# Six weight buffers laid 96 bytes out of step in a hybrid decoder block

## The chip, the cores and the metric

The kernel runs on one core of a Trainium2 chip. The metric is the device time of one execution in microseconds: the median of three runs. TensorE (PE) multiplies; VectorE (DVE), ScalarE (ACT) and GpSimd (POOL) do the elementwise work; SyncE (SP), ACT and POOL issue DMA transfers. On-chip memory (SBUF) has 128 partitions, and each tile takes the same bytes of every partition, so an address here is a byte within a partition.

## The reference

One layer of a decoder for 512 tokens and 16 meta tokens of width 1024, all in float32. A normalised input goes through one wide projection; its parts feed a gated linear attention (GLA) and a state space layer (S5), whose outputs are gated, merged and projected; a squared-ReLU MLP follows.

```python
xn = rmsnorm(h, g_mix_pre[l])
proj = xn @ w_in[l]                       # 1024 x 6160
...
y_gla = o @ w_o_gla[l]
...
glu = g_s @ w_glu[l] + b_glu[l]
y_ssm = glu[..., :D_MODEL] * jax.nn.sigmoid(glu[..., D_MODEL:])
mixed = jax.nn.sigmoid(z_gla) * y_gla + jax.nn.sigmoid(z_ssm) * y_ssm
h = h + rmsnorm(mixed @ w_out[l], g_mix_post[l])
hn = rmsnorm(h, g_ffn_pre[l])
f = jnp.square(jax.nn.relu(hn @ w_ff1[l])) @ w_ff2[l]
h = h + rmsnorm(f, g_ffn_post[l])
```

## The kernel before

Most products are done in three passes of TensorE's one-pass float32 type (`float32r`): each operand is split into a high part and a remainder, and `mm3` adds high x high, high x remainder and remainder x high into one PSUM bank. The weights go through a chain of three kinds of buffers, three of each, in the pool `wp`: a DMA on SP brings a block of 4 KB per partition into `wraw`, ScalarE rounds it into `whi` (`split_hi`), VectorE subtracts and writes the remainder to `wlo`. A block is 8 x 128 columns of a weight matrix (`raw_w`, `split_w_hi`, `split_w_lo`, `load_w`), or, in the last stage, 2 x 512 (`operands`).

PE works on such a block in one of two ways.

- *Weights held.* `feat_tile` calls `mm3` with `whi[:, k]` or `wlo[:, k]`, 128 columns, as the operand that is loaded into the array (LDWEIGHTS in the profile) and streams the inputs past it: `rh`/`rl` (the first u projections), `xh`/`xl` (the rest of the input projection), `ogh`/`ogl` (GLA output), `gh`/`gl` (S5's GLU), `hh`/`hl` (MLP, first product). The order per k is `whi` with the high part, `whi` with the remainder, `wlo` with the high part. A matmul streams 512 columns, or 256 and 272 where the tokens go in two halves (`HALVES`).
- *Weights moving.* In the MLP's second product (`step`, `product`) the activations `fh`/`fl` are held and 512 columns of `whi` or `wlo` stream past.

`w_out` has buffers of its own (`woh`, `wol`) and takes only `wraw` from the chain.

Where a tile lies follows from its pool. `wp` is the second pool on the left side of SBUF; all left-side pools opened later (`px`, `pg`, `pgl`'s counterpart `pw`, `pff`, `pw2` and others) lie above it, and the right-side pools grow down from the top. In pools made with `padded=True`, `mk` rounds every tile up to `LINE` = 64 floats, 256 bytes; `lead` and `tail` bring the two sides to a multiple of 256 at their start. In the program as built, the three `wraw`, the three `whi` and the three `wlo` buffers follow each other at distances of exactly 4096 bytes and all start at a multiple of 256. So do `xh`, `xl`, `ogh`, `ogl`, `gh`, `gl`, `hh`, `hl`, `mh`, `ml`, `woh`, `wol`, `fh` and `fl`, and every slice of 128 columns or of one k in them. `rh` and `rl` start 192 bytes past a multiple of 256, and so does each of their k.

```python
LINE = 64
raw = mk(wp, [P, kt, P], tag="wraw", bufs=3)
hi = mk(wp, [P, raw.shape[1], P], F32R, tag="whi", bufs=3)
lo = mk(wp, [P, raw.shape[1], P], F32R, tag="wlo", bufs=3)
```

PE's order is mostly written out by hand (`pinned`), and around it the S5 and GLA work of the other engines is interleaved. POOL's queue carries DMAs that go around the core's DRAM, and in it, at line 812, the fill of `zpad` (zeros for a padded kernel table) and, at line 1552, the loads of `w2raw` (blocks of the second MLP matrix, of which VectorE forms sums for the last stage).

Of the kernel before, what the change touches and what calls it, by code (L numbers as in the profile page):

```python
# [9 lines left out]
F32 = mybir.dt.float32  # L10
F32R = mybir.dt.float32r
# [6 lines left out]
P = 128  # L18
D = 1024
KT = D // P  # L20
# [11 lines left out]
LINE = 64  # L32
# [18 lines left out]
def hybrid_block(ctx: ExitStack, tc: tile.TileContext, io, out: bass.AP):  # L51
# [17 lines left out]
    count = [0]  # L69
# [11 lines left out]
    def mk(pool, shape, dt=F32, tag=None, **kw):  # L81
        count[0] += 1
        name = f"{tag or 'x'}_{count[0]}"
        size = 1
        for n in shape[1:]:
            size *= n
        if pool not in lined or size % LINE == 0:
            return pool.tile(shape, dt, tag=tag or name, name=name, **kw)
        t = pool.tile([shape[0], -(-size // LINE) * LINE], dt, tag=tag or name, name=name, **kw)[:, :size]
        if len(shape) == 2:  # L90
            return t
        dims = " ".join("abcd"[: len(shape) - 1])
        return t.rearrange(f"p ({dims}) -> p {dims}", **dict(zip("abcd", shape[1:])))

    def f32(t):
        return t.bitcast(F32)

    def pool(name, bufs=1, space=None, stack=None, side="left", padded=False):
        kw = {"side": side} if space is None else {"space": space}
        if space != DRAM:  # L100
            kw["reuse_waits"] = "tile"
        made = (stack or ctx).enter_context(tc.tile_pool(name=name, bufs=bufs, **kw))
        if padded:
            lined.append(made)
        return made

    cst = pool("cst", padded=True)
    wp = pool("wp", padded=True)
    dr = pool("dr", space=DRAM)
    ps_mm = pool("ps_mm", bufs=4, space=PSUM)  # L110
# [48 lines left out]
    def split_hi(dst, src, scale=1.0):  # L159
        S.activation(dst, src, AF.Copy, scale=scale)  # L160

    def raw_w(src):

        kt, n = src.shape[0] // P, src.shape[1]
        raw = mk(wp, [P, kt, P], tag="wraw", bufs=3)
        return nc.sync.dma_start(raw[:, :, :n], src.rearrange("(k p) n -> p k n", p=P)), raw

    def split_w_hi(raw):
        hi = mk(wp, [P, raw.shape[1], P], F32R, tag="whi", bufs=3)
        split_hi(hi, raw)  # L170
        return hi

    def split_w_lo(raw, hi):
        lo = mk(wp, [P, raw.shape[1], P], F32R, tag="wlo", bufs=3)
        V.tensor_sub(lo, raw, f32(hi))  # L175
        return lo

    def split_w(raw):
        hi = split_w_hi(raw)
        return hi, split_w_lo(raw, hi)  # L180
# [298 lines left out]
    def busy(n, cols=256):  # L479

        for _ in range(n):
            PE.matmul(idle[:, :cols], ones[:, :P], ones[:, :cols], start=True, stop=True)
# [8 lines left out]
    for kind, i in (("h", 0), ("h", 4), ("a", 0), ("u", 2), ("x", 0), ("x", 1), ("x", 2), ("x", 3), ("x", 4), ("u", 3), ("u", 4), ("w", 0), ("g", 0), ("u", 5), ("c", 0), ("u", 6), ("u", 7)):  # L491
        with behind():
# [15 lines left out]
            else:  # L508
                loaded, raw = raw_w(w_in[:, C_U + i * P : C_U + (i + 1) * P])
# [82 lines left out]

    uts = [u_tile() for _ in range(3)] + [mk(qc, [P, T8, NCK], tag=f"ut{i}") for i in (3, 4)]
    busy(5)
    w0, w1 = (tuple(mk(wp, [P, KT, P], F32R, tag=t, bufs=3) for t in ("whi", "wlo")) for _ in range(2))
    for k in range(KT):
        taken_raw(k, 0)
        for w, raw in zip((w0, w1), raws):
# [33 lines left out]
    low(0, (0, 2))  # L632
    raw_product(w3, 0, pair2[:, 256:], (3, lambda: spreads.append(spread(1))))
    w4_hi = split_w_hi(raws[4])
    high(0, range(4, 8))
    rows_of(1, spreads[1])
    w4 = w4_hi, split_w_lo(raws[4], w4_hi)
    low(0, (4, 6))
    last[3] = bank()
# [26 lines left out]
    late_take(3, 0)  # L666
    late_take(3, 1)
    f1_hi = split_w_hi(raws[6])
    late_take(4, 0)
    f1 = f1_hi, split_w_lo(raws[6], f1_hi)  # L670
    late_take(4, 1)
    sx.close()
# [734 lines left out]
    for c in range(0, D, 256):  # L1407
# [11 lines left out]
        for i, w in enumerate(load_w(wg[:, c : c + 256])):  # L1419
# [3 lines left out]
            t = mk(pgl, [P, SEQ], tag="ti", bufs=2)  # L1423
# [16 lines left out]
    for k in range(KT):  # L1440
        raw = mk(wp, [P, D], tag="wraw", bufs=3)
# [70 lines left out]
    w1 = io["w_ff1"][0]  # L1512
# [13 lines left out]
    f = mk(pff, [P, MF, SEQ], tag="f")  # L1526
# [67 lines left out]
    def operands(a, b, jj):  # L1594
        raw = mk(wp, [P, 2, 512], tag="wraw", bufs=3)
        nc.sync.dma_start(raw, b)
        bh, bl = (mk(wp, [P, 2, 512], F32R, tag=t, bufs=3) for t in ("whi", "wlo"))
        halved = S.activation(bh, raw, AF.Copy)  # L1598
        if later and jj % 2:
            with tc.issue_after(halved.ins):  # L1600
                nc.scalar.dma_start(*later.pop(0))
        V.tensor_sub(bl, raw, f32(bh))  # L1602
        ah, al = (mk(pff, [P, 2, HT], F32R, tag=t, bufs=3) for t in ("fh", "fl"))
        split_hi(ah, a)
        V.tensor_sub(al, a, f32(ah))
        return ah, al, bh, bl
# [20 lines left out]
    def product(acc, a, b, first, beside=None, last=False, closes=False):  # L1627
        held = []
        for jj in range(NJ // 2):
            ops = operands(a(jj), b(jj), jj)  # L1630
            if beside:
                beside(jj)
            if last and jj >= NJ // 2 - 2:
                held.append(ops)
                continue
            for t in range(2):
                step(acc, t, ops, first and jj == 0, jj == NJ // 2 - 1)
        return held
# [105 lines left out]
```

## Time and profile before

| | before |
|---|---|
| median of 3 runs | 875.06 us (874.87 to 875.43) |
| the profiled execution | 874.97 us |
| its span on the core, first to last instruction | 873.2 us, mean granted TensorE clock 0.998 |
| PE matmul busy | 862.7 us, 4824 instructions |
| PE weight loads busy | 738.3 us, 4824 |
| VectorE / ScalarE / POOL busy | 654.6 / 442.4 / 121.4 us |

The rows of the profile are read so: a group row has line, engine, operation, out<-in, for PE the size of the array used and the shape of the output, the count, then busy time and mean duration of one in ns, and the engine's idle time ahead with what ended it. A timeline row has start in us, duration in us, and the same names. A matmul's duration runs into the next one, so the distance between two starts is the time that one takes of PE. PE busy means matmuls; PEld are weight loads, which run beside them.

The stages by time: first projections with `rh`/`rl` to 38 us; input projection with `xh`/`xl` among S5 and GLA work to about 360 us; GLA output, GLU and `w_out` to 538 us; the MLP's first product to 712 us; its second to the end.

### The profile page before, as it was taken

What the parts mean: (1) busy time and instruction counts of PE and PEld (TensorE: products, weight loads), DVE (VectorE), ACT (ScalarE), POOL (GpSimd) and SP (SyncE); (2) the same over time, 40 slices, a digit from 0 to 9 for tenths busy, and PEclk for the clock granted to TensorE, in tenths of its full rate; (3) what the DMA queues carried; (4) which work ended last, traced back from release to release, by engine and by line L of the source; (5) the groups of instructions that cost most, each with busy time, mean ns of one, the idle gap of its engine ahead of it and who ended that gap; (6) DMA issues with size and microseconds to landing.
All of it is one profiled execution on the core that took longest, in us unless ns stands there. A gap on an engine that the chain in (4) does not pass through costs nothing.

```text
span 873.2 us, 13275 instructions
## 1 busy us (share of the span) xinstructions
PE 862.7 (99%) x4824; PEld 738.3 (85%) x4824; DVE 654.6 (75%) x1181; ACT 442.4 (51%) x749; POOL 121.4 (14%) x213
## 2 busy tenths in 40 slices
PE   9999999999999999999999999999999999999996
PEld 8998889898988888888888889888888888888884
DVE  7999889979686699855446656576766677688886
ACT  7677456676763554334333544333222236665763
POOL 1123021130303222241000001011111100000001
PEclk9999999999999999999999999999999999999999
DMA  9777766545455747658545842498989966755464
GB/s 315 235 228 230 209 140 162 168 137 158 113 145 160 242 133 208 209 151 298 155 147 174 238 132 100 142 352 291 320 289 341 320 224 232 272 195 198 169 199 140
DMA packets 166905, 180.57 MB, mean 207 GB/s; under 512 B 18056, under 2 KB 126760, under 8 KB 166840
## 3 DMA queue, kind: packets, MB, share of 16 engines
q1 hardware_dynamic: 146832, 115.95, 44.6%
q0 software_dynamic: 17744, 58.52, 19.8%
q10 hardware_dynamic: 2264, 5.25, 1.9%
q8 instruction: 38, 0.62, 0.3%
q14 instruction: 27, 0.22, 0.1%
HBM read 143.74 MB, written 35.95 MB: 206 GB/s over the span
## 4 chain that ended last, share of the span: by engine, by line
PE 95%; DVE 3%; ACT 1%; issue 0%; ACTq 0%; DVEq 0%
PE mm L61 70%; PE sm L61 23%; PE sm L66 2%; DVE wlo L79 1%; DVE M L79 0%; DVE c L1665 0%; ACT whi L79 0%; DVE xT L79 0%; ACTq L79 0%; ACT vs L79 0%; DVE vs L79 0%; DVE c L1659 0%; DVE d L79 0%; DVE mta L79 0%; ACT L79 0%
## 5 line engine op out<-in xcount | busy, mean ns | idle before, releaser
L160 ACT ACTIVATE whi<-wraw 128x1024 fp32r<-128x1024 f32 x82 | 86.9, 1059 | 210.6 <-PE mm L61 191.8
L175 DVE TENSOR_TENSOR wlo<-wraw,whi 128x1024 fp32r<-128x1024 f32 x82 | 100.3, 1223 | 98.2 <-ACT whi L160 98.0
L61 PE MATMUL mm<-xh,whi 128*128 128x512 f32 (+2 forms) x464 | 158.9, 342 | 0.0
L61 PE MATMUL mm<-xh,wlo 128*128 128x512 f32 (+2 forms) x464 | 155.9, 336 | 0.0
L61 PE MATMUL mm<-xl,whi 128*128 128x512 f32 (+2 forms) x464 | 155.6, 335 | 0.0
L61 PE MATMUL mm<-hh,whi 128*128 128x512 f32 (+1 forms) x280 | 104.0, 371 | 0.0
L61 PE MATMUL mm<-hl,whi 128*128 128x512 f32 (+1 forms) x280 | 103.8, 371 | 0.0
L61 PE MATMUL mm<-hh,wlo 128*128 128x512 f32 (+1 forms) x280 | 103.8, 371 | 0.0
L61 PEld LDWEIGHTS mm<-xh,whi 128*128 128x128 f32 x464 | 87.6, 189 | 9.5 <-issue 1.0
L61 PEld LDWEIGHTS mm<-xh,wlo 128*128 128x128 f32 x464 | 87.5, 189 | 9.0
L61 PEld LDWEIGHTS mm<-xl,whi 128*128 128x128 f32 x464 | 87.6, 189 | 8.4
L1602 DVE TENSOR_TENSOR wlo<-wraw,whi 128x1024 fp32r<-128x1024 f32 x56 | 68.4, 1223 | 20.1 <-ACT whi L1598 20.1
L61 PE MATMUL sm<-wlo,fh 128*128 128x512 f32 x192 | 74.8, 390 | 0.0
L61 PE MATMUL sm<-whi,fl 128*128 128x512 f32 x192 | 74.7, 389 | 0.0
L61 PE MATMUL sm<-whi,fh 128*128 128x512 f32 x192 | 74.7, 389 | 0.0
L1598 ACT ACTIVATE whi<-wraw 128x1024 fp32r<-128x1024 f32 x56 | 58.6, 1049 | 16.8 <-PE mm L61 11.7
L61 PEld LDWEIGHTS mm<-hh,whi 128*128 128x128 f32 x280 | 52.8, 188 | 9.1
L61 PEld LDWEIGHTS mm<-hh,wlo 128*128 128x128 f32 x280 | 52.7, 188 | 9.0
L61 PEld LDWEIGHTS mm<-hl,whi 128*128 128x128 f32 x280 | 52.8, 188 | 9.0
L160 ACT ACTIVATE fh<-f 128x512 fp32r<-128x512 f32 x48 | 30.3, 631 | 45.5 <-PE sm L61 30.3
L61 PE MATMUL mm<-gh,whi 128*128 128x512 f32 x128 | 49.8, 389 | 0.0
L61 PE MATMUL mm<-gl,whi 128*128 128x512 f32 x128 | 49.8, 389 | 0.0
(445 smaller groups left out, 1787.6 us busy)
## 6 DMA issues: line engine op xcount, KB each, us to landing
wraw<-in_w_ff_dram SPq DMA_DIRECT2D x56, 512.0 KB, 4.7
wraw<-in_w_in_dram SPq DMA_DIRECT2D x46, 512.0 KB, 4.1
w2raw<-in_w_ff_dram POOLq DMA_DIRECT2D x16, 1024.0 KB, 8.6
t2d<-w2t POOLq DMA_DIRECT2D x16, 1024.0 KB, 5.7
wraw<-t2d SPq DMA_DIRECT2D x32, 512.0 KB, 3.9
wraw<-in_w_glu_dram SPq DMA_DIRECT2D x16, 512.0 KB, 4.3
M<-kpad POOLq DMA_DIRECT2D x64, 64.0 KB, 3.1
wraw<-in_w_o_gla_dram SPq DMA_DIRECT2D x8, 512.0 KB, 6.1
```

The costliest lines, as they stand in the source:

```text
L61: ins = nc.tensor.matmul(*args, **kw)
L66: ins = nc.tensor.transpose(*args, **kw)
L79: return lambda *args, **kw: tc.keep_in_program_order(getattr(self.engine, name)(*args, **kw))
L160: S.activation(dst, src, AF.Copy, scale=scale)
L175: V.tensor_sub(lo, raw, f32(hi))
L1598: halved = S.activation(bh, raw, AF.Copy)
L1602: V.tensor_sub(bl, raw, f32(bh))
```

## The change

The six buffers `whi` and `wlo` get 24 floats (96 bytes) more each, of which nothing is used; a helper `weights` makes them and hands out the first 1024 floats, so that shapes, operations and operands stay as they were. The buffers now lie 4192 bytes apart: `whi` at 0, 96 and 192 and `wlo` at 32, 128 and 224 modulo 256. The buffer of `whi` and that of `wlo` which belong to the same block are always 288 bytes, 32 modulo 256, apart in phase. A tile `fill` of 48 floats makes the 6 x 96 bytes up to 768, three times 256, so that what lies above `wp` on the left side moves by 768 bytes and keeps its phase; the right side does not move.

The order of the instructions on each engine is the same as before. Two waits on POOL are new, since tiles of the left side that moved now overlap in place with tiles of other times: the fill of `zpad` also waits for PE's last reading of `rl`, and the second load of `w2raw` for ScalarE's writing of `gh` instead of being covered by other waits.

```diff
+    STAGGER = 24
+
+    def weights(tag, shape=(KT, P)):
+
+        count[0] += 1
+        a, b = shape
+        t = wp.tile([P, a * b + STAGGER], F32R, tag=tag, name=f"{tag}_{count[0]}", bufs=3)
+        return t[:, : a * b].rearrange("p (a b) -> p a b", a=a)
+
...
     def split_w_hi(raw):
-        hi = mk(wp, [P, raw.shape[1], P], F32R, tag="whi", bufs=3)
+        hi = weights("whi")
...
     def split_w_lo(raw, hi):
-        lo = mk(wp, [P, raw.shape[1], P], F32R, tag="wlo", bufs=3)
+        lo = weights("wlo")
...
-    w0, w1 = (tuple(mk(wp, [P, KT, P], F32R, tag=t, bufs=3) for t in ("whi", "wlo")) for _ in range(2))
+    w0, w1 = (tuple(weights(t) for t in ("whi", "wlo")) for _ in range(2))
+    wp.tile([P, 3 * LINE - 6 * STAGGER], F32, tag="fill", name="fill")
...
-        bh, bl = (mk(wp, [P, 2, 512], F32R, tag=t, bufs=3) for t in ("whi", "wlo"))
+        bh, bl = (weights(t, (2, 512)) for t in ("whi", "wlo"))
```

## Prediction

> **What bounds the kernel now.** I read the page's busy times and its chain of waits first. TensorE's matmul row is busy for 862.7 of 873.2 us at a granted clock that is full in every slice, and the chain that ends last lies on PE for 95% of the span.
>
> ```profile
> PE 862.7 (99%) x4824; PEld 738.3 (85%) x4824; DVE 654.6 (75%) x1181; ACT 442.4 (51%) x749; POOL 121.4 (14%) x213
> PE   9999999999999999999999999999999999999996
> PEclk9999999999999999999999999999999999999999
> PE 95%; DVE 3%; ACT 1%; issue 0%; ACTq 0%; DVEq 0%
> ```
>
> So only what changes the step from one matmul to the next can change the time by more than a little. The change does not reorder or add an instruction; it moves addresses. The question is therefore how often PE works on the moved buffers, in which shapes, and whether its step depends on where they lie. The groups by shape give the counts; each form stands once for `whi` with the high part, and two more of the same count go with it (remainder of the input, and `wlo`).
>
> ```profile
> L61 PE MATMUL mm<-hh,whi 128*128 128x512 f32 x232 | 90.3, 389 | 0.0
> L61 PE MATMUL mm<-xh,whi 128*128 128x512 f32 x224 | 89.1, 398 | 0.0
> L61 PE MATMUL mm<-gh,whi 128*128 128x512 f32 x128 | 49.8, 389 | 0.0
> L61 PE MATMUL mm<-ogh,whi 128*128 128x512 f32 x64 | 25.5, 399 | 0.0
> L61 PE MATMUL sm<-whi,fh 128*128 128x512 f32 x192 | 74.7, 389 | 0.0
> L61 PE MATMUL mm<-whi,fh 128*128 128x512 f32 x32 | 12.4, 389 | 0.0
> L61 PE MATMUL mm<-xh,whi 128*128 128x256 f32 x120 | 35.3, 294 | 0.0
> L61 PE MATMUL mm<-xh,whi 128*128 128x272 f32 x120 | 34.5, 287 | 0.0
> L61 PE MATMUL mm<-hh,whi 128*128 128x256 f32 x48 | 13.7, 286 | 0.0
> L61 PEld LDWEIGHTS mm<-hh,whi 128*128 128x128 f32 x280 | 52.8, 188 | 9.1
> ```
>
> Wide (512 columns), weights held in the array: 3 x (232 + 224 + 128 + 64) = 1944. Wide, with the weights streaming and `fh`/`fl` held (the second MLP product): 3 x (192 + 32) = 672. Narrow: 3 x (120 + 48) = 504 of 256 columns and 3 x 120 = 360 of 272.
>
> A matmul's own duration overlaps the next one's, so what counts is start to start, from the timeline of PE. First and last rows of three undisturbed stretches with 256 columns; in the first, inputs and weights all lie at multiples of 256 bytes; in the other two `rh` and `rl` lie 192 bytes past one, and the weights at one.
>
> ```profile
> 155.99 0.28 PE L61 MATMUL mm<-xh,wlo 128*128 128x256 f32 x1
> ...
> 157.43 0.28 PE L61 MATMUL mm<-xh,wlo 128*128 128x256 f32 x1
> ...
> 32.66 0.28 PE L61 MATMUL sm<-rh,whi 128*128 128x256 f32 x1
> ...
> 35.37 0.28 PE L61 MATMUL sm<-rh,wlo 128*128 128x256 f32 x1
> ...
> 11.36 0.28 PE L61 MATMUL sm<-rh,wlo 128*128 128x256 f32 x1
> ...
> 12.38 0.28 PE L61 MATMUL mm<-rh,wlo 128*128 128x256 f32 x1
> ```
>
> Twelve steps in 1.44 us are 120.0 ns; 23 steps in 2.71 us are 117.8; nine in 1.02 us are 113.3. Same shape, same clock: the step does depend on how weights and moving input lie to each other, and all at the same phase is the worst of the three. The same with 272 columns, aligned first:
>
> ```profile
> 45.14 0.29 PE L61 MATMUL mm<-xh,whi 128*128 128x272 f32 x1
> ...
> 48.02 0.29 PE L61 MATMUL mm<-xh,wlo 128*128 128x272 f32 x1
> ...
> 29.70 0.29 PE L61 MATMUL sm<-rh,whi 128*128 128x272 f32 x1
> ...
> 32.54 0.28 PE L61 MATMUL sm<-rh,wlo 128*128 128x272 f32 x1
> ```
>
> 23 steps each: 2.88 us are 125.2 ns, 2.84 us are 123.5. For 512 columns the trace has only the aligned case, 132 steps here:
>
> ```profile
> 609.97 0.39 PE L61 MATMUL mm<-hh,wlo 128*128 128x512 f32 x1
> ...
> 639.89 0.39 PE L61 MATMUL mm<-hh,wlo 128*128 128x512 f32 x1
> ```
>
> 29.92 us over 132 are 226.7 ns. A weight load of 188 ns, which runs beside the matmul ahead, has 39 ns to spare in such a step and none in one of 113 to 120; that is a reason why a hindered load could show in the narrow shapes alone.
>
> The Trainium skill speaks against any effect: TensorE: Matmul & The Clock Gate, Step-by-step: what each phase is for, says that PE has two independent SBUF read ports, so that loading the next weights takes no read bandwidth from the running matmul. By it the change is worth nothing. The three steps of 113, 118 and 120 ns do not agree with it as it stands.
>
> **The change part by part.** (1) *Narrow matmuls.* After it the six buffers lie at 0, 96 and 192 (`whi`) and 32, 128 and 224 (`wlo`) modulo 256, the inputs still at 0. One of six keeps the old relation, and none has exactly the one of `rh` that the trace shows, so I bound by its rows. At 256 columns the gain per step is between 120.0 - 117.8 = 2.2 and 120.0 - 113.3 = 6.7 ns: 1.1 to 3.4 us over 504. I take the middle, 4.4 ns, 2.2 us, since both speeds stand in the trace for the very same offset. At 272 columns it is 125.2 - 123.5 = 1.7 ns, 0.6 us over 360; below nothing is not excluded for an offset that is no multiple of 64, and I take 0.6. Together 2.8 us. These lie on the chain (PE's rows above), so the end moves with them.
>
> (2) *Wide matmuls, weights held.* No row has another offset, so the price per step is open on both sides. Below: nothing shows a step under 226.7, and the spare 39 ns say that the load is hidden. Above: right after PE turns from transposes to wide matmuls, the first steps are out of their even pace. The groups of two short windows, from 292.5 to 293.0 us just behind such a turn (two rows) and from 293.2 to 293.6 (the last row), give what that costs.
>
> ```profile
> L61 PE MATMUL mm<-xl,whi 128*128 128x512 f32 x1 | 0.4, 395 | 0.0
> L61 PE MATMUL mm<-xh,wlo 128*128 128x512 f32 x1 | 0.4, 393 | 0.0
> ...
> L61 PE MATMUL mm<-xh,wlo 128*128 128x512 f32 x1 | 0.4, 389 | 0.0
> ```
>
> 395 and 393 against 389 are 5 ns. If weights at several phases kept PE out of its pace everywhere, that is 1944 x 5 = 9.7 us. I take nothing, because the pace is regained within three steps whatever came ahead, and keep +9.7 us as the end.
>
> (3) *Wide matmuls, weights moving.* 672 at the same bounds, 0 to 3.4 us; I take 0. The narrow stretches above, with a moving input 192 past a line, were no slower than the aligned one. The Trainium skill (SBUF — State Buffer, Specifications (TRN2)) has lines of 16 bytes, of which 96 is a multiple; by it no moving read crosses a line more than before and this term is 0. No run here shows an offset of 32 in such a matmul.
>
> (4) *ScalarE and VectorE* write these buffers. The group that writes `wlo` sat idle 98 us ahead of its 82 instructions, 1.2 us each, waiting for ScalarE, which in turn waits for PE to free a buffer; a few per cent more per instruction would be covered by that, so I take nothing.
>
> ```profile
> L175 DVE TENSOR_TENSOR wlo<-wraw,whi 128x1024 fp32r<-128x1024 f32 x82 | 100.3, 1223 | 98.2 <-ACT whi L160 98.0
> L160 ACT ACTIVATE whi<-wraw 128x1024 fp32r<-128x1024 f32 x82 | 86.9, 1059 | 210.6 <-PE mm L61 191.8
> ```
>
> (5) *768 bytes more* on the left side make two pairs of tiles overlap, so POOL gets two waits more: the fill of `zpad` now also waits for the readers of `rl`, the second load of `w2raw` for ScalarE's writes of `gh`.
>
> ```profile
> 38.20 0.29 PE L61 MATMUL sm<-rl,whi 128*128 128x272 f32 x1
> ...
> 43.29 0.87 POOL L812 MEMSET zpad<- 128x896 f32 x1
> ```
>
> The last matmul on `rl` starts at 38.20 us, and the fill came at 43.29 behind other work of its queue. The load of `w2raw` ahead of the second one in that queue waits for matmuls on `wol`, which come later than anything of `gh`. Both waits are met ahead of time: nothing, and what is queued behind them on POOL stays where it is.
>
> Sum: -2.2 - 0.6 + 0 + 0 + 0 = -2.8 us. The profiled execution took 874.97 us (span 873.2 and 1.8 around it), 0.09 under the median of 875.06. 874.97 - 2.8 = 872.2 us.
>
> **The rivals.** *No effect* (chance 0.15): PE's pace is set elsewhere and the three speeds are a matter of what else runs at 11, 33 and 156 us. For it: two speeds at one offset. Against it: the aligned rows never fall to 113. Time 875.0; the Trainium skill's two ports, above, would give the same.
>
> *The wide matmuls lose their even pace* (0.32), the slow side. Place: the 1944 wide matmuls with weights held. Mechanism: within one tile the loads go `whi`, `whi`, `wlo`, now 32 modulo 256 apart where before all had one phase, so that two of every three loads meet a change of phase; each costs up to the 5 ns of a step out of pace: 1296 x 5 = 6.5 us, 874.97 - 2.8 + 6.5 = 878.7. It decides from 2.8 us / 1944 = 1.4 ns a wide step on. For it: the even pace, which the aligned run holds for hundreds of steps and a turn to transposes breaks. Against it: the spare 39 ns.
>
> *The wide step falls too* (0.05). From 256 to 512 columns the aligned step grows by 226.7 - 120.0 = 106.7 ns, so both hold 120.0 - 106.7 = 13.3 ns that do not grow with the columns, and the fast narrow step holds 113.3 - 106.7 = 6.6. If the wide one loses the same 6.7, it is 1944 x 6.7 = 13.0 us: 874.97 - 2.8 - 13.0 = 859.2. Against it stands a wide matmul at 826.44 us with no load beside it, since the next one waited until 826.80:
>
> ```profile
> L61 PE MATMUL sm<-whi,fh 128*128 128x512 f32 x1 | 0.4, 388 | 0.0
> ...
> 826.80 0.19 PEld L61 LDWEIGHTS sm<-wlo,fh 128*128 128x128 f32 x1 [0.40 <-DVE wlo L1602]
> ```
>
> It lasted 388 ns, 1 less than with a load beside it. That the change does not do what it says is no case: the offsets follow from the sizes, and the fill keeps the rest at 256.
>
> **How the numbers follow.** The forecast, a small gain in the narrow shapes alone, has 0.48; its own range, from the bounds of (1), is 871.0 (3.4 and 0.6 off) to 873.3 (1.1 and 0.6 off). The predicted time is its 872.2. The range is to leave out 0.2: the rival at 859.2 (0.05) is left out below, and above the dearer half of the slow rival; so 868.0, the whole of the narrow gain (3.4 and 0.6) and near a quarter of the wide one, to 880.0, a little over the slow rival's 878.7. A measurement of this kernel can tell 0.2%, 1.75 us. Faster by more than that: 0.43 of the forecast's 0.48, and the wide rival's 0.05: 0.48. Within: 0.15 and the forecast's other 0.05: 0.20. Slower: 0.32.
>
> **What would show it.** In the changed profile's timeline, `xh`/`xl` stretches with 256 columns should step at 113 to 118 ns where 120 stood, those with 272 at 123 to 124, and stretches like the one from 610 to 640 us still at 226.7 (132 steps in 29.92 us). Means of 256-column groups fall from 283 towards 278. A wide step of 228 or more, or means of 391 and over in the `hh` groups, would show the slow rival; a rise in `sm<-whi,fh` alone would show term (3). The prediction is wrong if the narrow stretches keep 120 ns, or if any wide group's mean moves from 389.

## The result and the profile after

| | before | with the change |
|---|---|---|
| median (four runs each, side by side) | 875.00 us (874.87 to 875.43) | 887.88 us (887.47 to 888.62) |
| ratio | | 1.0147, 95% interval 1.013 to 1.0165 |
| the profiled execution, its span | 874.97, 873.2 us | 887.81, 886.0 us |

The kernel became slower by 12.9 us, 1.5%, far over what a measurement can tell, and past 880.0, the upper end of the range. The page of the changed kernel shows the same picture as before, only longer: the granted clock is full in every slice, VectorE and ScalarE work as long as they did (their groups that write the weights have the old 1223 and 1059 ns each), and PE alone has grown, by 875.6 - 862.7 = 12.9 us.

```profile
PE 875.6 (99%) x4824; PEld 739.0 (83%) x4824; DVE 655.3 (74%) x1181; ACT 442.1 (50%) x749; POOL 121.4 (14%) x213
...
PEclk9999999999999999999999999999999999999999
...
PE 92%; DVE 3%; DMA 2%; ACT 1%; issue 0%; ACTq 0%; SPq 0%; DVEq 0%
...
L169 ACT ACTIVATE whi<-wraw 128x1024 fp32r<-128x1024 f32 x82 | 86.9, 1059 | 219.3 <-PE mm L61 204.4
L184 DVE TENSOR_TENSOR wlo<-wraw,whi 128x1024 fp32r<-128x1024 f32 x82 | 100.3, 1223 | 103.5 <-ACT whi L169 103.0
```

Where PE grew is read from the starts of its stages. The timeline of before has these first matmuls: input projection, S5's GLU, `w_out`, the MLP's first product, its second, and the very last matmul.

```profile
38.45 0.28 PE L61 MATMUL mm<-xh,wa 128*32 128x256 f32 x1
...
403.04 0.39 PE L61 MATMUL mm<-gh,whi 128*128 128x512 f32 x1
...
490.08 0.39 PE L61 MATMUL mm<-woh,mh 128*128 128x512 f32 x1
...
535.42 0.28 PE L61 MATMUL mm<-hh,whi 128*128 128x256 f32 x1
...
712.20 0.39 PE L61 MATMUL sm<-whi,fh 128*128 128x512 f32 x1
...
864.56 0.39 PE L61 MATMUL sm<-whi,fl 128*128 128x512 f32 x1
```

The same matmuls in the timeline of the changed kernel:

```profile
39.16 0.28 PE L61 MATMUL mm<-xh,wa 128*32 128x256 f32 x1
...
406.83 0.39 PE L61 MATMUL mm<-gh,whi 128*128 128x512 f32 x1
...
495.83 0.40 PE L61 MATMUL mm<-woh,mh 128*128 128x512 f32 x1
...
541.20 0.28 PE L61 MATMUL mm<-hh,whi 128*128 128x256 f32 x1
...
721.24 0.40 PE L61 MATMUL sm<-whi,fh 128*128 128x512 f32 x1
...
877.74 0.39 PE L61 MATMUL sm<-whi,fl 128*128 128x512 f32 x1
```

The differences of the gaps: 0.7 us more in the first projections, 3.1 in the input projection with the GLA output, 2.0 in the GLU, 0.0 in `w_out`, 3.3 in the first product, 4.1 in the second. The one stage that does not use `whi` and `wlo` is the one that did not change.

The groups by shape show which matmuls it is. In the prediction the wide `hh`, `gh` and `fh` groups stood at 389 ns and the 256-column group of `xh` at 294.

```profile
L61 PE MATMUL mm<-hl,whi 128*128 128x512 f32 x232 | 91.9, 396 | 0.0
L61 PE MATMUL mm<-hh,whi 128*128 128x512 f32 x232 | 91.5, 394 | 0.0
L61 PE MATMUL mm<-hh,wlo 128*128 128x512 f32 x232 | 91.0, 392 | 0.0
...
L61 PE MATMUL sm<-wlo,fh 128*128 128x512 f32 x192 | 76.2, 397 | 0.0
L61 PE MATMUL sm<-whi,fh 128*128 128x512 f32 x192 | 76.1, 396 | 0.0
...
L61 PE MATMUL mm<-gh,whi 128*128 128x512 f32 x128 | 50.5, 394 | 0.0
...
L61 PE MATMUL mm<-xh,whi 128*128 128x256 f32 x120 | 35.1, 293 | 0.0
```

The wide groups shown rose by 3 to 7 ns, in both uses of the weights, and the narrow one fell by 1. The timeline shows the steps. The first pair of rows is the stretch of 132 wide steps that took 29.92 us before, then the one of 12 steps with 256 columns (1.44 us before) and the one of 23 with 272 (2.88 before).

```profile
616.72 0.39 PE L61 MATMUL mm<-hh,wlo 128*128 128x512 f32 x1
...
647.31 0.39 PE L61 MATMUL mm<-hh,wlo 128*128 128x512 f32 x1
...
157.45 0.28 PE L61 MATMUL mm<-xh,wlo 128*128 128x256 f32 x1
...
158.87 0.28 PE L61 MATMUL mm<-xh,wlo 128*128 128x256 f32 x1
...
45.84 0.28 PE L61 MATMUL mm<-xh,whi 128*128 128x272 f32 x1
...
48.72 0.29 PE L61 MATMUL mm<-xh,wlo 128*128 128x272 f32 x1
```

30.59 us over 132 are 231.7 ns on average where 226.7 stood; 1.42 over 12 are 118; 2.88 over 23 are the old 125.2.

For the whole run I took the distance from each matmul's start to the next one's, for all neighbours of the float32r kind with 128 columns held, without those above 253 ns (wide), 153 (272 columns) or 146 (256 columns), which hold a pause. These means of steps are used in all that follows:

| steps | counted | before, ns | after, ns | difference, us |
|---|---|---|---|---|
| 512 columns, weights held | 1897 | 227.1 | 231.8 | +8.9 |
| 512 columns, weights moving | 670 | 226.7 | 233.1 | +4.3 |
| 512 columns, `woh`/`wol` (not moved) | 188 | 226.9 | 227.0 | 0.0 |
| 256 columns on `xh`, `xl`, `hh`, `hl` | 489 | 119.6 | 118.1 | -0.7 |
| 272 columns on `xh`, `xl` | 346 | 125.4 | 125.4 | 0.0 |
| 256 and 272 columns on `rh`, `rl` | 101 and 119 | 116.3, 123.5 | 118.7, 125.9 | +0.5 |

They add up to 13.0 us, all of the loss.

### The profile page after: what moved, and what is told of

It reads as the page before. It is cut to its first block, busy times and chain, and to the rows that moved or that the text cites. A ratio compares the mean times of both kernels' runs of the same rounds, so it can differ in the third digit from the quotient of the medians.

```text
span 886.0 us, 13276 instructions
## 1 busy us (share of the span) xinstructions
PE 875.6 (99%) x4824; PEld 739.0 (83%) x4824; DVE 655.3 (74%) x1181; ACT 442.1 (50%) x749; POOL 121.4 (14%) x213
## 4 chain that ended last, share of the span: by engine, by line
PE 92%; DVE 3%; DMA 2%; ACT 1%; issue 0%; ACTq 0%; SPq 0%; DVEq 0%
PE mm L61 68%; PE sm L61 22%; PE sm L66 2%; DMA wraw<-in_w_in_dram 1%; DMA xT<-in_x_cols_dram 1%; DVE wlo L79 1%; DVE M L79 0%; DVE c L1675 0%; ACT whi L79 0%; ACTq L79 0%; ACT vs L79 0%; DVE c L1669 0%; DVE vs L79 0%; DVE d L79 0%; DVE mta L79 0%
## 5 line engine op out<-in xcount | busy, mean ns | idle before, releaser
L169 ACT ACTIVATE whi<-wraw 128x1024 fp32r<-128x1024 f32 x82 | 86.9, 1059 | 219.3 <-PE mm L61 204.4
L184 DVE TENSOR_TENSOR wlo<-wraw,whi 128x1024 fp32r<-128x1024 f32 x82 | 100.3, 1223 | 103.5 <-ACT whi L169 103.0
```

## The experiments

"Distance" below is the address of a weight buffer less that of the input used with it, modulo 256. Before, it is 0 for every wide matmul. A "phase" is an address modulo 256 by itself, a "triple" the three products of one k, and a "tile" of steps the 24 matmuls (8 triples) that work on one block of weights.

**Is it the phases at all?** The change also sets the buffers further apart, moves what lies above and adds two waits. In this kernel, and in every later one that is built on the change, every buffer gets 64 spare floats (4352 bytes apart, a multiple of 256), and a list says at which float of it a tile starts.

```diff
-    STAGGER = 24
+    SPARE = 64
+    PHASE = {"held": {"whi": [0, 0, 0], "wlo": [0, 0, 0]}, "moving": {"whi": [0, 0, 0], "wlo": [0, 0, 0]}}
+    taken = {"whi": 0, "wlo": 0}
...
-    def weights(tag, shape=(KT, P)):
+    def weights(tag, shape=(KT, P), moving=False):
...
-        t = wp.tile([P, a * b + STAGGER], F32R, tag=tag, name=f"{tag}_{count[0]}", bufs=3)
-        return t[:, : a * b].rearrange("p (a b) -> p a b", a=a)
+        t = wp.tile([P, a * b + SPARE], F32R, tag=tag, name=f"{tag}_{count[0]}", bufs=3)
+        at = PHASE["moving" if moving else "held"][tag][taken[tag] % 3]
+        taken[tag] += 1
+        return t[:, at : at + a * b].rearrange("p (a b) -> p a b", a=a)
...
-    wp.tile([P, 3 * LINE - 6 * STAGGER], F32, tag="fill", name="fill")
...
-        bh, bl = (weights(t, (2, 512)) for t in ("whi", "wlo"))
+        bh, bl = (weights(t, (2, 512), moving=True) for t in ("whi", "wlo"))
```

> Six buffers 4352 bytes apart (4096 and 256 spare), every one used from its start, so all phases are 0 modulo 256 as before; 1536 bytes move what lies above. If phases alone matter: 875.0 us within 0.2%, wide steps 226.7 ns. If the distance from 4096, or the shift of the left side with its two POOL waits, costs the time: near 887.9.

874.71 us, ratio 0.9995 (0.9985 to 1.0004), and all means of the table as before to 0.1 ns, but for 0.3 ns on `rh`. Buffers further apart and a shift of the tiles above (1536 bytes here, 768 in the change) cost nothing. The two waits cost nothing in the change itself either: its fill of `zpad` starts 0.6 us later than before (43.9 against 43.3 us) and its second load of `w2raw` 5.8 us later (546.7 against 540.9), no more than the 0.7 and 5.8 us by which PE is behind there. What is left of the change is its phases.

**Do the loads have to differ among themselves?** The prediction's slow rival blamed the change of phase from one load to the next. These two give all six buffers one phase, 96 and 64:

```diff
-    PHASE = {"held": {"whi": [0, 0, 0], "wlo": [0, 0, 0]}, "moving": {"whi": [0, 0, 0], "wlo": [0, 0, 0]}}
+    PHASE = {"held": {"whi": [24, 24, 24], "wlo": [24, 24, 24]}, "moving": {"whi": [24, 24, 24], "wlo": [24, 24, 24]}}
...
+    PHASE = {"held": {"whi": [16, 16, 16], "wlo": [16, 16, 16]}, "moving": {"whi": [16, 16, 16], "wlo": [16, 16, 16]}}
```

> As c0, but all six buffers are used from byte 96 on, so that weights share one phase, which is not the inputs'. Theory 'change of phase from load to load': back to 875 or a little less (narrow steps 113 to 118: 872 to 875). Rival 'phase between weights and inputs': 886 to 890, wide steps 231 to 234. Rival 'a start that is no multiple of 64': 886 to 890 as well.

> As all96, with 64 bytes in place of 96. Theory 'change of phase from load to load': 872 to 875. Rival 'phase between weights and inputs': 886 to 890. Rival 'a start that is no multiple of 64': 872 to 875, which tells it from the second by all96 against this.

All at 96: 891.25 us, ratio 1.018 (1.0165 to 1.0195), slower than the change. All at 64: 887.80 us, 1.0143 (1.0126 to 1.016). With no change of phase between loads the wide steps are 234.2 and 233.3 ns with weights held, the same for all three products of a triple, and 233.3 and 232.2 with weights moving. So a change of phase is not needed for the loss, and by itself that mechanism falls. The third idea, a start that is no multiple of 64, falls with the second kernel, where every start is one. The kernel with 96 came out 1.25 us above its expected range, 886 to 890. The groups of the kernel with 64 by shape:

```profile
L61 PE MATMUL mm<-hh,whi 128*128 128x512 f32 x232 | 91.4, 394 | 0.0
...
L61 PE MATMUL mm<-xh,whi 128*128 128x256 f32 x120 | 34.8, 290 | 0.0
...
L61 PE MATMUL mm<-xh,whi 128*128 128x272 f32 x120 | 34.3, 286 | 0.0
```

The narrow groups did fall here, from 294 to 290 and from 287 to 286; in steps, 256 columns gained 3.75 ns (1.8 us) and 272 columns 1.9 ns (0.7 us). The prediction's gain in the narrow shapes is there, 2.5 us, and is buried under 15.5 us from the wide ones.

**One load of three out of step.** Phase 0 for `whi`, 32 for `wlo`:

```diff
-    PHASE = {"held": {"whi": [0, 0, 0], "wlo": [0, 0, 0]}, "moving": {"whi": [0, 0, 0], "wlo": [0, 0, 0]}}
+    PHASE = {"held": {"whi": [0, 0, 0], "wlo": [8, 8, 8]}, "moving": {"whi": [0, 0, 0], "wlo": [8, 8, 8]}}
```

> whi at phase 0, wlo at 32, in all three buffers: the phase changes twice in every three steps, and nothing else of the change is there. Theory 'change of phase from load to load': 884 to 888, with the triple of 232, 240 and 228 ns in the wide held steps. Rival 'phase between weights and inputs': a third of the loads are off, 878 to 881. Rival 'a start that is no multiple of 64': 878 to 881 too.

890.75 us, 1.0175 (1.0159 to 1.019), more than any of the three had expected. The groups by shape:

```profile
L61 PE MATMUL mm<-hl,whi 128*128 128x512 f32 x232 | 92.8, 400 | 0.0
L61 PE MATMUL mm<-hh,whi 128*128 128x512 f32 x232 | 91.6, 395 | 0.0
L61 PE MATMUL mm<-hh,wlo 128*128 128x512 f32 x232 | 90.3, 389 | 0.0
```

The matmul of the remainder (`hl,whi`) is the one beside which the displaced `wlo` is loaded, and it has the longest step, 238.8 ns; the one that then works with `wlo` has 228.4; the next, whose own weights and whose neighbour's lie at distance 0, still has 232.6. A triple takes 699.8 ns on `hh`, 700.0 in the kernel with all at 64, 680.1 before. One load in three at 32 costs as much as three at 64: the loss is no fixed price per displaced load, and it goes on into a step whose two buffers are both at 0. The pattern of the triple is the one expected from a change of phase (232, 240 and 228). The two kernels before show that a loss needs no such change, but that it adds to the price of the distance is not excluded: no kernel has all six buffers at 32.

**Address or distance?** 64 bytes more at the bottom of SBUF move the weights and all that is laid out from the left (`xh`, `ogh`, `mh`, `fh`), not what is laid out from the right (`gh`, `hh`). The first kernel is that, the second moves both sides.

```diff
-LEAD = 32
+LEAD = 48
...
-TAIL = 56
+TAIL = 40
```

> The kernel before, with 64 bytes more at the bottom of SBUF: the weights, and with them the inputs xh, xl, ogh, mh and the operands of the last product, move by 64 bytes against a 256-byte grid; gh, gl, hh and hl, which are laid out from the top, stay. Theory 1 (what costs is a distance between the addresses of the weights and of the inputs streaming beside them that is no multiple of 256): wide steps on xh, ogh and of the last product stay at 226.5 to 228 ns, the 384 on gh and the 696 on hh go to 233 to 234 ns (+6.2 ns each, +6.7 us), the 144 narrow ones on hh lose 0.3 us: 881 to 883 us. Theory 2 (what costs is the address of the weights itself, when it is no multiple of 256): all wide steps go to 232 to 234 ns, 887 to 890 us. Theory 3 (the change of phase from load to load, all that the prediction allowed for): nothing changes, 875 us.

> The kernel before with everything moved by 64 bytes: weights and inputs from the bottom by 64 up, inputs laid out from the top by 64 up too. Theory of the distance: all wide steps at 226.5 to 228 ns, narrow ones as before, 874.5 to 875.5 us. Theory of the address itself (weights off the 256-byte grid): 887 us or more.

Left side alone: 882.89 us, 1.009 (1.0073 to 1.0107). Both sides: 875.95 us, 1.0007 (0.9998 to 1.0017), no difference that can be told, with all means of the table as before to 0.1 ns. The groups of the first by shape:

```profile
L61 PE MATMUL mm<-hh,whi 128*128 128x512 f32 x232 | 91.4, 394 | 0.0
...
L61 PE MATMUL sm<-whi,fh 128*128 128x512 f32 x192 | 74.7, 389 | 0.0
...
L61 PE MATMUL mm<-gh,whi 128*128 128x512 f32 x128 | 50.4, 394 | 0.0
L61 PE MATMUL mm<-xh,whi 128*128 128x256 f32 x120 | 35.3, 294 | 0.0
```

Only the stages whose inputs stayed have slowed: wide steps on `gh` and `hh` are 233 to 234 ns, those on `xh` 227.5, in the second product 226.8. What counts is the distance of the weights to the input beside them, and the address by itself does nothing. The Trainium skill (SBUF — State Buffer, Who interferes with whom) says that of the engines' ports only the pair that VectorE and GpSimd share causes contention, so that PE waits on no one; by that the first of these kernels would take 875 us, and its time and its `gh` and `hh` groups do not agree. That the slower steps are a wait for a port is not shown.

**Do the two uses add up?** The change's own phases where the weights are held, and 0 in the last product; then the other way round.

```diff
-    PHASE = {"held": {"whi": [0, 0, 0], "wlo": [0, 0, 0]}, "moving": {"whi": [0, 0, 0], "wlo": [0, 0, 0]}}
+    PHASE = {"held": {"whi": [0, 24, 48], "wlo": [8, 32, 56]}, "moving": {"whi": [0, 0, 0], "wlo": [0, 0, 0]}}
...
+    PHASE = {"held": {"whi": [0, 0, 0], "wlo": [0, 0, 0]}, "moving": {"whi": [0, 24, 48], "wlo": [8, 32, 56]}}
```

> The change's phases only where the weights are held in TensorE's array (every product but the last); in the last product's operands all phases are 0. If the shares add up as the trace of the change has them (wide held steps +8.9 us, narrow -0.7 us, first product +0.5 us): 883.5 to 885 us, with the last product's steps back at 226.7 ns. If the last product's share is a consequence of what goes before it: its steps stay at 232 to 234 ns, 887 us or more.

> The change's phases only in the last product, where the weights are the streaming operand and the activations fh and fl, at phase 0, are loaded; phases 0 everywhere else. If the shares add up: the last product's 670 steps at 232 to 234 ns (+4.3 us), all else as before, 879 to 880.5 us. If a phase of the streaming operand alone costs nothing and the loss there was carried over: 875 us.

883.40 us, 1.0094 (1.0079 to 1.0109), and 878.19 us, 1.0035 (1.0022 to 1.0048). Held alone, the last product's group `sm<-whi,fh` is back at 389 ns; moving alone, it is at 394 and the `hh` groups at 389. Each use pays for itself. Both times lie a little under their expected ranges (883.5 and 879). 8.4 + 3.1 us are 11.5 of the 12.9. Half of the rest, 0.7 us, is in the last product, whose 670 steps were 232.1 ns alone and 233.1 in the change, for which I have no cause.

**Which distances are free?** High part and remainder share a phase, 16, 128 and 192 by turns.

```diff
-    PHASE = {"held": {"whi": [0, 0, 0], "wlo": [0, 0, 0]}, "moving": {"whi": [0, 0, 0], "wlo": [0, 0, 0]}}
+    PHASE = {"held": {"whi": [4, 32, 48], "wlo": [4, 32, 48]}, "moving": {"whi": [4, 32, 48], "wlo": [4, 32, 48]}}
```

> High part and remainder of a tile share a phase; the three pairs of buffers lie at phases 16, 128 and 192. If only a distance of 0 is free, all wide steps read 231 to 235 ns at each of the three, 887 to 892 us. If half the period is free as well, the third of the tiles at 128 reads 227 ns, 884 to 887 us; if a shift within 16 or 32 bytes changes nothing, the third at 16 does. Narrow steps (256 columns on xh, 119.5 before): by the phases 64 to either side, which gave 115.1 (weights 64 above the input) and 116.3 (the first product before, weights 64 above rh), 192 gives 115 to 118; 128 gives 117 to 119, 16 between 117 and 120.

885.84 us, 1.0122 (1.0107 to 1.0137). The time lies under the 887 expected for one free distance and would fit half the period being free as well; the steps say otherwise. Wide steps on `xh`: 230.5 ns at 16, 232.4 at 128, 229.6 at 192; on `hh`: 233.4, 232.4 and 229.2. The distance of 128 is nearly as dear as 64, and 192 loses least. With 256 columns, steps on `xh` read 118.4, 119.2 and 117.8 ns.

The mean of 230.5 at 16 hides two speeds. The buffers go round in the order in which the tiles use them, so each tile's distance is known: of the 27 wide tiles at 16, seven step at 226.7 to 226.9 ns, as at distance 0, and twenty at 233.2 to 233.5. Both speeds occur on the same input. These are the first and last rows of two such tiles, each of 24 matmuls without a pause:

```profile
410.83 0.39 PE L61 MATMUL mm<-gh,whi 128*128 128x512 f32 x1
...
416.04 0.40 PE L61 MATMUL mm<-gh,wlo 128*128 128x512 f32 x1
...
427.35 0.40 PE L61 MATMUL mm<-gh,whi 128*128 128x512 f32 x1
...
432.72 0.39 PE L61 MATMUL mm<-gh,wlo 128*128 128x512 f32 x1
```

5.21 us over 23 steps are 226.5 ns, 5.37 over 23 are 233.5, with the same distance, input and shape. So what a step takes is no function of the distance alone; a tile keeps one of two paces, and what chooses is open.

**A version that keeps the gain alone.** Every tile at distance 0, but 64 for the 18 tiles that meet 256 or 272 columns of `xh` and `hh`. `split_w_hi` and `split_w_lo` get the start as an argument, the narrow entries of the list of work carry a mark, and `narrow()` gives 16 floats for them; the second kernel goes round 8, 12 and 20.

```diff
+    NARROW = [16]
+    drawn = [0]
+
+    def narrow():
+        drawn[0] += 1
+        return NARROW[drawn[0] % len(NARROW)]
...
-    def load_w(src):
+    def load_w(src, narrows=False):
...
-        return [split_w(raw_w(src[:, c : c + P])[1]) for c in range(0, src.shape[1], P)]
+        return [split_w(raw_w(src[:, c : c + P])[1], narrow() if narrows else 0) for c in range(0, src.shape[1], P)]
...
-    ws = load_w(w1[:, : EARLY * P])
+    ws = load_w(w1[:, : EARLY * P], True)
```

> Only the tiles that are used against narrow inputs (256 or 272 columns of xh, xl, hh and hl; 18 tiles) lie 64 bytes above their inputs; every other tile is at distance 0, the last product too. Theory of the distance: all wide steps stay at 226.5 to 228 ns; the 350 counted narrow steps of 256 columns on xh go from 119.5 to 115.1 ns (-1.6 us), the 138 on hh from 119.7 to 117.9 (-0.25 us), the 346 of 272 columns from 125.4 to 123.5 (-0.7 us): 2.5 us less, 872.2 to 873.2 us against 875.0. If a tile's distance also costs its wide neighbours (the load that goes beside the last matmul of the tile ahead), 1 in 24 of the wide steps may rise, at most 0.3 us. Rival: the narrow gain is given back at the waits on evictions behind these tiles, 875 us.

> As the version with 64 bytes in the narrow tiles alone, but their distance goes round 48, 80 and 32 bytes. If the gain of a narrow step grows smoothly toward 64: 48 and 80 read 115 to 117 ns on xh with 256 columns, 32 reads 117 to 118; the time lies 0.5 to 1 us above the version with 64, 872.8 to 874. If 64 is special (its own grid of 64 bytes), all three read 117.5 to 119, 874 to 875 us.

With 64: 872.80 us, ratio 0.9972 (0.996 to 0.9983), faster than both kernels. Its groups by shape:

```profile
L61 PE MATMUL mm<-hh,whi 128*128 128x512 f32 x232 | 90.3, 389 | 0.0
...
L61 PE MATMUL mm<-xh,whi 128*128 128x256 f32 x120 | 34.9, 291 | 0.0
...
L61 PE MATMUL mm<-xh,whi 128*128 128x272 f32 x120 | 34.4, 286 | 0.0
```

In steps, 256 columns went from 119.6 to 116.4 ns (-1.6 us) and 272 from 125.4 to 123.5 (-0.7 us), wide ones stayed at 227.1: 2.2 us by the steps, 2.35 by the medians (875.15 to 872.80). With 48, 80 and 32: 874.79 us, 0.9992 (0.9983 to 1.0001), no difference that can be told; on `xh`, 256 columns read 118.9, 118.9 and 118.3 ns, and 272 columns lost 1.0 ns. The gain does not grow smoothly toward 64; of the distances tried, 64 alone has it in both shapes (96 has 123.5 ns at 272 columns, but 117.8 at 256).

## Why the prediction was wrong

**The step that failed is term (2),** with (3) behind it. "(2) *Wide matmuls, weights held* ... I take nothing", with 9.7 us kept as the end: it measured +8.9. "(3) ... I take 0", bounds 0 to 3.4 us: it measured +4.3, out of its bounds. The two are the whole of the loss, 13.2 us. Two reasons led to the nothing of (2), and both fall:

- *"The spare 39 ns say that the load is hidden."* The load's own row shows no hindrance: before and after, a load lasts 188 ns, inside a step of 232. The step grew all the same, so the spare time says nothing about it.

```profile
L61 PEld LDWEIGHTS mm<-hh,whi 128*128 128x128 f32 x280 | 52.6, 188 | 10.5
```

- *"The pace is regained within three steps whatever came ahead."* That was read where all distances are 0. In the change the old pace does not come back, and every tile has a buffer off distance 0 in it. The 132-step stretch shows it: 231.7 ns on average over five and a half tiles.

Term (3) was put at 0 because narrow stretches with a shifted moving input were no slower. The kernel with phases in the last product alone has 232.1 ns there, where 226.7 stood: the narrow shapes did not speak for the wide one.

**What the views of before could have shown.** The trace had the two narrow shapes at two distances and the wide one at 0 alone. I took nothing for the shape that had no row, and so the sign of the narrow shapes became the sign of the sum. The runs show the opposite sign: at distance 64, 256 columns gain 3.75 ns a step and 512 lose 6.2 (all at 64). For 1944 + 672 wide matmuls against 864 narrow ones, an unknown of either sign in the wide step had to carry the estimate.

**Term (1)** was -2.8 us. Its mechanism stands: the kernel with 64 in the narrow tiles alone gains 2.35 us. In the change itself it brought 0.7, because its six phases hold no distance of 64, and those that they hold read 117 to 119 ns at 256 columns. And one part was missing: `rh` and `rl` take their weights from the same buffers. Before, weights lay 64 above them (0 less 192, modulo 256), the good distance; the change took it away, 0.5 us by the steps, 0.7 by the stage. The prediction saw two speeds, 113.3 and 117.8 ns, at that one distance and took the middle. All at 64 has the same two, by whole tiles: on `xh`, 113.3 to 114.3 and 117.6 to 117.9. What comes ahead has a part in it: three of these tiles (in the kernel before at 99.0, 105.6 and 134.8 us) step at 113.7 to 113.8 with everything at 64, and at 117.7 to 117.9 with 64 in the narrow tiles alone.

**Terms (4) and (5)** were right: the writers' rows kept their durations, and the first experiment shows that the moved tiles and the waits cost nothing.

**The rivals.** *No effect* and *the wide step falls too* are out. *The wide matmuls lose their even pace* had the right place and sign; its price, 5 ns for two loads of three, gave 878.7, and the time was 887.9. Its mechanism is not needed: with one phase for all loads, steps are as slow. Distance to the input takes its place, and it touches the moving use too, which that rival left out. The idea of a pace that is lost as a whole, though, fits the kernel with `wlo` at 32, where one load in three costs as much as three, and the two paces at 16. The Trainium skill's two read ports (TensorE: Matmul & The Clock Gate, Step-by-step: what each phase is for), weighed in the prediction, would leave every step as it was: over the distances tried, no shape agrees.

**What stays open** is how the distance acts, and what chooses between two paces at one distance. That the load reads beside the running matmul fits the 238.8 ns of the step that has the displaced load beside it. It may not be all: a wide matmul of the changed kernel at 305.82 us has no load beside it in the timeline of the weight loads, since the next one starts at 306.15,

```profile
305.59 0.19 PEld L61 LDWEIGHTS mm<-xh,wlo 128*128 128x128 f32 x1
306.15 0.26 PEld L61 LDWEIGHTS sm<-M,BA 128*32 128x32 f32 x10 [0.36 <-issue]
```

and still the groups of the window from 305.8 to 306.2 us give it 398 ns,

```profile
L61 PE MATMUL mm<-xh,wlo 128*128 128x512 f32 x1 | 0.4, 398 | 0.0
```

where the same one before, at 303.48 us, has 388 in the groups of the window from 303.46 to 303.86 us:

```profile
L61 PE MATMUL mm<-xh,wlo 128*128 128x512 f32 x1 | 0.4, 388 | 0.0
```

The profile models the end of a matmul, so these 10 ns are weak evidence; the next matmul, though, also starts 8 ns later after it than before (327 against 319 ns). Whether its own load or the pace of the steps ahead of it does this was not told apart.

## What to carry to other kernels

Treat the addresses of the two operands of a matmul as a pair: where the kernel is bound by PE, read the step from start to start for each shape, tile by tile, since a mean can hide two speeds, and compare shapes that meet at different distances modulo 256. Before moving a buffer, list every use of it by shape with its count; a gain seen in one shape says nothing of the sign in another, and the shape with most matmuls sets the time. If a distance helps one shape, give it to the tiles of that shape alone.

## What was not expected of the hardware

- Float32r matmuls of 512 columns with 128 held step at 226.7 ns where weights and input lie at distance 0 modulo 256, and between 228 and 239 ns, on average over a group, at nearly all others tried (16, 64, 96, 128, 192, and 32 for `wlo` alone). One group reads 227.0 off 0, `hh` with `whi` at 192, but its triple takes 687.6 ns against 680.1. At 16, seven tiles of 27 keep the pace of distance 0 from end to end.
- With 256 columns 0 is the worst distance: 119.6 ns, against 115.1 at 64 on `xh` with all at 64 (115.8 where only narrow tiles were moved) and 117.8 to 119.2 at the other distances. With 272 columns 0 has 125.4, 64 and 96 have 123.5, and 128 and 192 with 126.5 to 126.6 are worse than 0.
- Distance is not the whole of it. At 64, tiles of 256 columns on `xh` step at either about 113.8 or about 117.8 ns, and those on `hh` all at 117.8; the mean of 115.1 on `xh` is of both kinds. A tile can have the one pace in one kernel and the other in the next, at the same distance.
